# Three products of a hybrid decoder layer turned: weights as the 512-column moving operand, results turned back by TensorE transposes

## The chip, the core and the metric

The kernel runs on one NeuronCore of a Trainium2 chip. The metric is device time in microseconds for one execution; the figure for a kernel is the median of its runs. Before the change three runs took 1487.34, 1488.31 and 1488.09 us, median 1488.09 us.

## What is computed

One decoder layer in float32, for 256 tokens of width 2048. Attention runs inside one block of 256 tokens, with 8 heads of 128; the reference, cut to what matters here:

```python
h = rms_norm(r, g_mix)
z = h @ w_in                                   # 2048 x 10240
q, k, v, c_b, c_c, c_x, g_a, g_c = split(z)    # six of 1024 columns, two of 2048
attn = moba_attention(rms_norm(q), rms_norm(k), v)
y_attn = attn @ w_attn_out                     # 1024 x 2048
y_conv = (c_b * causal_depthwise_conv(c_c * c_x, w_conv)) @ w_conv_out
merged = sigmoid(g_a) * y_attn + sigmoid(g_c) * y_conv
r = r + merged @ w_o                           # 2048 x 2048
h = rms_norm(r, g_mlp)
r = r + square(relu(h @ w_up)) @ w_down        # 2048 x 8192, 8192 x 2048
h = rms_norm(r, g_ple)
r = r + sigmoid(h @ w_ple_gate) * (p @ w_ple_proj)
```

## The kernel before

A float32 product is made from three passes: weights and activations are each split into a high part (a rounding write, ScalarE, L87) and a low part (VectorE subtracts, L88), and TensorE adds up high times high, high times low and low times high.

Weights come from HBM in **units** of 128 x 2048 floats (1 MB), one DMA each on the SyncE queue (`load_unit`, L119), into three `raw` buffers. A unit is split in two halves of 1024 columns; `w_hi` and `w_lo` have seven half-unit buffers each. A unit is what 16 pairs of 128 x 128 weight tiles need.

There are two forms of product.

- `cols` (L155 to L160) keeps features on partitions. A tile of 128 weight columns is stationary. For each of its 16 steps `mm` issues a **pair**: the high weights over [x_hi | x_lo], 512 columns (L150, the last step L153), and the low weights over x_hi, 256 columns (L151). One bank then holds two parts of a result of 128 features x 256 tokens, which `total` or `add_to_r` adds up.
- `rows` (L127 to L143) keeps tokens on partitions. The activations are stationary and the split weights move, 512 columns in each instruction: three matmuls (L139, L140, L141) for each of 16 steps and each of two halves of the tokens, so 96 for a **chunk** of 512 weight columns. The result is two banks of 128 tokens x 512 features.

Before the change `rows` makes q, k and v (six chunks, about the first 147 us), and `cols` all else, in this order: convolution inputs (`ps_conv`), for each of 16 tiles the two gates and the two branch outputs (`ps_g`, `ps_y`), w_o (`ps_o`), then four times a quarter of w_up (`ps_up`) and of w_down (`ps_dn`), at last the per-layer gate (`ps_pg`, `ps_proj`).

In the gate stage a gate's tile is added up by ScalarE and VectorE (L163, L164), multiplied by the norm's row (L343) and put through the sigmoid (L344); a branch output is added up the same way and multiplied by its gate (L352); the two are added (L354) and split into the operand `mT` of w_o (L87, L88). For w_down `add_to_r` adds both parts of each tile to the residual `r` on VectorE (L363, 128 instructions for the four quarters).

Six PSUM banks serve the products (`acc`) and two the small work of attention, such as transposes (`trp`, tag `tr`). Functions in the list `pending` are called between weight units of a product (`run_pending`); attention's pieces, one group of four transposes (`tr_qk`, L263) and others, run in that way within the q, k and v products. The framework's scheduler fixes the order on each engine when the program is built, and each engine then runs its instructions in that order.

Of the kernel before, what the change touches and what calls it, by code (L numbers as in the profile page):

```python
# [29 lines left out]
# Rows of the packed per-channel vectors, as columns after the load.  # L30
# [5 lines left out]
def hybrid_block_kernel(ctx: ExitStack, tc: tile.TileContext, ins: dict, out: bass.AP):  # L36
    """A float32 matrix product runs as three float32r passes: each operand is the exact sum of a
    high and a low part of 12 bits (a float32r write rounds to the high one), and
    hi*hi + hi*lo + lo*hi leaves out only what lies below float32's last bit.

    q, k and v come out with tokens on partitions: weights are the moving operand. All else is kept
    transposed, features on partitions: a tile of 128 weight columns is the stationary operand, its
    high part over [x_hi | x_lo] (512 columns), its low part over x_hi. A norm's 1/rms is applied to a
    product's result, its gain to the operand."""
# [31 lines left out]
    def col(i):  # L76
        return vec[:, i:i + 1]

    def rsqrt_mean(dst, sumsq, n, k):
        """dst = (sumsq / n + eps) ** -0.5 on [128, k]."""  # L80
        nc.vector.tensor_scalar(dst, sumsq, 1.0 / n, EPS, op0=ALU.mult, op1=ALU.add)
        nc.gpsimd.tensor_tensor(dst, dst, half[:, :k], op=ALU.pow)

    def split(hi, lo, src, gain=None):
        """hi + lo = src * gain, exactly."""
# [7 lines left out]
    def xsplit(xs, k, src, gain=None):  # L93
        """xs[k] = [hi | lo] of 128 features."""
# [21 lines left out]
    def load_unit(w):  # L116
        """A unit of 128 x 2048 weights, split, in halves."""
# [9 lines left out]
    def rows(wname, c, xs, name, load=load_unit, pops=1):  # L127
        """Two banks: [256 tokens, 512] of xs @ w, chunk c of w's columns."""
        w = ins[wname]
        nu = w.shape[1]  # L130
        ps = [bank(f"ps_{name}_{t}") for t in range(NT)]
        for u in range(nu):
            wt = load(w[c, u])
# [10 lines left out]

    def mm(ps, wt, i, x, first, last):
        """Tile i of a unit's 16 against x: ps[:, :256] += hi * hi, ps[:, 256:] += the cross products."""
# [8 lines left out]
    def cols(wt, xs, name, at=0, nk=16):  # L155
        """One bank: two parts of [128, 256 tokens] of (xs @ w) transposed."""
        ps = bank(f"ps_{name}")
        for k in range(nk):
            mm(ps, wt, at + k, xs[k], k == 0, k == nk - 1)
        return ps  # L160
# [40 lines left out]
    def load_first(w):  # L201
        """A unit of weights and as much of x, in the order in which the first product needs them."""
# [100 lines left out]
    for c in range(2):  # L303
        if c == 0:
            ps_q = rows("w_qkv", 0, xT, "q0", load_first)
            x_stats()
            ps_k = rows("w_qkv", 2, xT, "k0", pops=3)
            qs[c], ks[c] = qk_evac(ps_q, "q0"), qk_evac(ps_k, "k0")
        else:
            qs[c] = qk_evac(rows("w_qkv", 1, xT, "q1"), "q1")  # L310
            ks[c] = qk_evac(rows("w_qkv", 3, xT, "k1"), "k1")
        vs[c] = tokens(rows("w_qkv", 4 + c, xT, f"v{c}"), f"v{c}")
# [24 lines left out]
    mT = {}  # L337
    for n in range(16):
        gates = []
        for i in range(2):  # L340
            g = temp(f"g{i}")
            total(g, cols(load_unit(w_in[24 + 16 * i + n]), xT, f"g{i}_{n}"))
# [163 lines left out]
```

## Time and profile before

| what | value |
|---|---|
| runs | 1487.34, 1488.31, 1488.09 us; median 1488.09 |
| span of the profiled execution | 1486.1 us |
| the profiled execution's own time | not listed apart; by the median of the runs, 2.0 us lie outside the span |
| TensorE busy | 1475.5 us, 99% |
| VectorE busy | 959.9 us, 65% |
| ScalarE busy | 755.5 us, 51% |
| DMA | 278.46 MB, mean 187 GB/s |
| granted TensorE clock | 1.000 |

The span runs from the first to the last instruction. A TensorE record is longer than the distance to the next one's start, because matmuls overlap; what a matmul costs in a stream is the distance from start to start. Busy time is the union of the records.

### The profile page before, as it was taken

How to read it: one execution, taken by the hardware profiler on the slowest of the kernel's cores; microseconds unless marked ns; L12 is line 12 of the kernel's file. 1: busy time of each engine (PE TensorE's matmuls, PEld its weight loads, DVE VectorE, ACT ScalarE, POOL GpSimd, SP SyncE). 2: the span in 40 equal slices, each digit the busy share in tenths (PEclk: the TensorE clock that was granted, in tenths of full speed). 3: DMA queues.
4: the chain of work that ended last, by engine and by line, in shares of the span. 5: the costliest groups of instructions: out<-in, count | busy, mean ns of one | idle time of the engine just before them, and what ended most of it. 6: DMA issues, size and time to landing. Idle time of an engine off the chain costs nothing.

```text
span 1486.1 us, 20573 instructions
## 1 busy us (share of the span) xinstructions
PE 1475.5 (99%) x8216; PEld 1275.9 (86%) x8216; DVE 959.9 (65%) x1352; ACT 755.5 (51%) x1135; POOL 11.2 (1%) x27
## 2 busy tenths in 40 slices
PE   8999999999999999999999999999999999999998
PEld 6888888888888888888888888888888888888887
DVE  7555676766666666666655666556665566677775
ACT  7655555455555544445543455334553345554543
POOL 0100000000000000000000000000000000000000
PEclk9999999999999999999999999999999999999999
DMA  8545444454545556454545555454555555455551
GB/s 314 225 170 181 173 177 176 173 187 181 198 172 197 180 189 246 180 189 178 198 174 195 180 189 189 180 198 173 196 179 189 189 180 198 173 195 185 191 199 57
DMA packets 44304, 278.46 MB, mean 187 GB/s; under 512 B 5040, under 2 KB 7344, under 8 KB 11952
## 3 DMA queue, kind: packets, MB, share of 16 engines
q1 hardware_dynamic: 44064, 277.11, 51.5%
q8 instruction: 65, 1.06, 0.3%
q14 instruction: 31, 0.25, 0.0%
q10 hardware_dynamic: 144, 0.04, 0.0%
HBM read 275.03 MB, written 2.10 MB: 186 GB/s over the span
## 4 chain that ended last, share of the span: by engine, by line
PE 99%; DMA 0%; DVE 0%; ACT 0%; issue 0%
PE ps_dn L150 15%; PE ps_up L150 15%; PE ps_dn L151 8%; PE ps_up L151 8%; PE ps_g L150 8%; PE ps_conv L150 6%; PE ps_g L151 4%; PE ps_o L150 4%; PE ps_pg L150 4%; PE ps_y L150 4%; PE ps_conv L151 3%; PE ps_o L151 2%; PE ps_pg L151 2%; PE ps_y L151 2%; PE ps_q L139 1%; PE ps_q L141 1%
## 5 line engine op out<-in xcount | busy, mean ns | idle before, releaser
L88 DVE TENSOR_TENSOR w_lo<-raw,w_hi 128x1024 fp32r<-128x1024 f32 (+1 forms) x524 | 632.2, 1208 | 281.8 <-ACT w_hi L87 272.9
L87 ACT ACTIVATE w_hi<-raw 128x1024 fp32r<-128x1024 f32 (+1 forms) x524 | 547.0, 1045 | 402.5 <-PE ps_dn L153 121.6
L150 PE MATMUL ps_up<-x,w_hi 128*128 128x512 f32 x960 | 341.7, 399 | 0.0
L150 PE MATMUL ps_dn<-x,w_hi 128*128 128x512 f32 x960 | 341.7, 399 | 0.0
L151 PE MATMUL ps_dn<-x,w_lo 128*128 128x256 f32 x1024 | 277.2, 281 | 0.0
L151 PE MATMUL ps_up<-x,w_lo 128*128 128x256 f32 x1024 | 277.1, 281 | 0.0
L150 PEld LDWEIGHTS ps_dn<-x,w_hi 128*128 128x128 f32 x960 | 180.4, 188 | 41.6
L150 PEld LDWEIGHTS ps_up<-x,w_hi 128*128 128x128 f32 x960 | 180.4, 188 | 41.5
L151 PEld LDWEIGHTS ps_dn<-x,w_lo 128*128 128x128 f32 x1024 | 193.3, 189 | 6.4
L151 PEld LDWEIGHTS ps_up<-x,w_lo 128*128 128x128 f32 x1024 | 193.3, 189 | 6.3
L150 PE MATMUL ps_g<-x,w_hi 128*128 128x512 f32 x480 | 170.9, 399 | 0.0
L151 PE MATMUL ps_g<-x,w_lo 128*128 128x256 f32 x512 | 138.6, 281 | 0.0
L150 PE MATMUL ps_conv<-x,w_hi 128*128 128x512 f32 x360 | 129.5, 402 | 0.0
L150 PEld LDWEIGHTS ps_g<-x,w_hi 128*128 128x128 f32 x480 | 90.2, 188 | 20.8
L151 PE MATMUL ps_conv<-x,w_lo 128*128 128x256 f32 x384 | 103.5, 280 | 0.0
L151 PEld LDWEIGHTS ps_g<-x,w_lo 128*128 128x128 f32 x512 | 96.7, 189 | 3.2
L163 ACT ACTIVATE a<-ps_up 128x256 f32<-128x256 f32 x64 | 24.6, 384 | 119.8 <-PE ps_up L153 119.8
L150 PE MATMUL ps_o<-x,w_hi 128*128 128x512 f32 x240 | 85.4, 399 | 0.0
L150 PE MATMUL ps_pg<-x,w_hi 128*128 128x512 f32 x240 | 85.4, 398 | 0.0
L363 DVE TENSOR_TENSOR r<-ps_dn,r 128x256 f32<-128x256 f32 x128 | 54.3, 424 | 42.9 <-PE ps_dn L153 40.7
L150 PEld LDWEIGHTS ps_conv<-x,w_hi 128*128 128x128 f32 x360 | 67.6, 188 | 15.3
L150 PE MATMUL ps_y<-x,w_hi 128*128 128x512 f32 x224 | 80.4, 398 | 0.0
(181 smaller groups left out, 1657.8 us busy)
## 6 DMA issues: line engine op xcount, KB each, us to landing
raw<-in_w_up_dram SPq DMA_DIRECT2D x64, 1024.0 KB, 4.8
raw<-in_w_down_dram SPq DMA_DIRECT2D x64, 1024.0 KB, 4.8
raw<-in_w_in_dram SPq DMA_DIRECT2D x56, 1024.0 KB, 4.8
raw<-in_w_qkv_dram SPq DMA_DIRECT2D x20, 1024.0 KB, 4.8
raw<-in_w_branch_dram SPq DMA_DIRECT2D x16, 1024.0 KB, 4.8
raw<-in_w_o_dram SPq DMA_DIRECT2D x16, 1024.0 KB, 4.8
raw<-in_w_ple_gate_dram SPq DMA_DIRECT2D x16, 1024.0 KB, 4.9
raw<-in_w_qkv_dram SPq DMA_DIRECT2D x16, 256.0 KB, 6.1
```

The lines of the kernel that those rows point to most:

```text
L87: nc.scalar.activation(hi, src, AF.Copy)
L88: nc.vector.tensor_sub(lo, src, hi.bitcast(F32))
L139: nc.tensor.matmul(ps[t], xh, hi, start=k == 0, stop=False)
L141: nc.tensor.matmul(ps[t], xl, hi, start=False, stop=k == KU * nu - 1)
L150: nc.tensor.matmul(ps, wh, both, start=first, stop=False)
L151: nc.tensor.matmul(ps[:, S:], wl, x[:, 0, :], start=False, stop=False)
L163: nc.scalar.activation(dst, ps[:, S:], AF.Copy)
L363: nc.vector.tensor_add(dst, ps[:, i * S:(i + 1) * S], dst)
```

## The change

The gates, the branch outputs and the product with w_down go from `cols` to `rows`. w_in, w_branch and w_down still lie in HBM as tiles of 128 columns, so a unit is now gathered from four neighbouring tiles, a quarter of each, by one DMA of 128 x 4 x 512 (`load_rows`), and split in four pieces of 512 columns: ScalarE and VectorE read four runs of 128 columns and write 512 in a row. The gates are read from PSUM by one sigmoid with the norm's factor as scale, tokens being on partitions; VectorE multiplies the branch outputs by them and adds. The merge is turned back by TensorE transposes (`transposed`, groups of four) and split into `mT` from PSUM. The four quarters of w_down add up in eight tiles `d`; after the last quarter `d` is transposed and added to `r`, and the operand `hP` and the sum of squares `ss2` follow. `cols` has a new argument `flush`: at step 12 of a tile the queued work is run, for the first tile of w_o and of the per-layer gate.

```diff
+    def load_rows(w):
+        raw = wp.tile([P, UNIT], F32, tag="raw", name="raw", bufs=3)
+        nc.sync.dma_start(raw.rearrange("p (n f) -> p n f", n=4), w.rearrange("n p f -> p n f"))
+        src = raw.rearrange("p (n k m) -> p k n m", n=4, k=KU)
+        halves = []
+        for h in range(2):
+            hi = wp.tile([P, HALF], F32R, tag="hi", name="w_hi")
+            lo = wp.tile([P, HALF], F32R, tag="lo", name="w_lo")
+            view = [t.rearrange("p (k n m) -> p k n m", n=4, k=2) for t in (hi, lo)]
+            for j in range(2):
+                split(view[0][:, j], view[1][:, j], src[:, 2 * h + j])
+            halves.append((hi, lo))
+        return halves
...
+    def tiles(wname, n, us=range(4)):
+        w = ins[wname]
+        return [lambda u=u: load_rows(w[n:n + 4, :, u * CW:(u + 1) * CW]) for u in us]
...
-    def cols(wt, xs, name, at=0, nk=16):
+    def cols(wt, xs, name, at=0, nk=16, flush=None):
         ps = bank(f"ps_{name}")
         for k in range(nk):
+            if k == flush:
+                run_pending(len(pending))
             mm(ps, wt, at + k, xs[k], k == 0, k == nk - 1)
...
+    def transposed(n, src, done):
+        ps = trp.tile([P, 2, S], F32, tag="tr", name=f"tr_{n}")
+        for i in range(2):
+            o = (n + i) % 4 * P
+            for t in range(NT):
+                nc.tensor.transpose(ps[:, i, t * P:(t + 1) * P], src[t][:, o:o + P], ident)
+        done(n, ps)
...
+    def split_m(n, ps):
+        for i in range(2):
+            xsplit(mT, n + i, ps[:, i, :])
+
+    for c in range(4):
         gates = []
         for i in range(2):
-            g = temp(f"g{i}")
-            total(g, cols(load_unit(w_in[24 + 16 * i + n]), xT, f"g{i}_{n}"))
-            nc.vector.tensor_mul(g, g, row0)
-            nc.scalar.activation(g, g, AF.Sigmoid)
+            ps = rows(tiles("w_in", 24 + 16 * i + 4 * c), xT, f"g{i}_{c}", pops=2)
+            g = [slot([P, CW], F32, f"g{i}_{c}_{t}") for t in range(NT)]
+            for t in range(NT):
+                nc.scalar.activation(g[t], ps[t], AF.Sigmoid, scale=st0["col"][:, t:t + 1])
             gates.append(g)
-            run_pending(len(pending))
-        wt = load_unit(ins["w_branch"][n])
-        parts = []
+        run_pending(len(pending))
         for i, xs in enumerate((attnT, convT)):
-            y = temp(f"y{i}")
-            total(y, cols(wt, xs, f"y{i}_{n}", at=8 * i, nk=8))
-            nc.vector.tensor_mul(y, y, gates[i])
-            parts.append(y)
-        nc.vector.tensor_add(parts[0], parts[0], parts[1])
-        xsplit(mT, n, parts[0])
+            ps = rows(tiles("w_branch", 4 * c, range(2 * i, 2 * i + 2)), xs, f"y{i}_{c}")
+            for t in range(NT):
+                nc.vector.tensor_mul(gates[i][t], ps[t], gates[i][t])
+        for t in range(NT):
+            nc.vector.tensor_add(gates[0][t], gates[0][t], gates[1][t])
+        for n in (4 * c, 4 * c + 2):
+            pending.append(lambda n=n, m=gates[0]: transposed(n, m, split_m))
...
-        add_to_r(n, cols(load_unit(ins["w_o"][n]), mT, f"o_{n}"))
+        add_to_r(n, cols(load_unit(ins["w_o"][n]), mT, f"o_{n}", flush=12))
...
+    def end_r(n, ps):
+        u = n // 2
+        nc.vector.tensor_add(r[u], ps, r[u])
+        for i in range(2):
+            xsplit(hP, n + i, r[u][:, i, :], col(G_PLE + n + i))
+        square_sum(ss2, u, r[u])
...
-        for n in range(16):
-            add_to_r(n, cols(load_unit(ins["w_down"][16 * q + n]), uT, f"dn_{q}_{n}"))
+        for c in range(4):
+            ps = rows(tiles("w_down", 16 * q + 4 * c), uT, f"dn_{q}_{c}")
+            for t in range(NT):
+                if q == 0:
+                    d[c, t] = slot([P, CW], F32, f"d_{c}_{t}")
+                    nc.scalar.activation(d[c, t], ps[t], AF.Copy)
+                else:
+                    nc.vector.tensor_add(d[c, t], ps[t], d[c, t])
             if q == 3:
-                xsplit(hP, n, r[n // 2][:, n % 2, :], col(G_PLE + n))
-                if n % 2 == 1:
-                    square_sum(ss2, n // 2, r[n // 2])
+                for n in (4 * c, 4 * c + 2):
+                    pending.append(lambda n=n, m=(d[c, 0], d[c, 1]): transposed(n, m, end_r))
...
-        gate = cols(wt, hP, f"pg_{n}")
+        gate = cols(wt, hP, f"pg_{n}", flush=12)
```

A group of four transposes turns 256 columns of both token halves. There are 16 groups: eight for the merge, eight for `d`. How the instructions then stand is shown at three places.

**ScalarE, at the end of a gate's product.** `w_hi<-raw` is a split of weights, `g` a gate; xN is a run of N like rows. Before, the last gate of tile 4 and the branch outputs behind it:

```order
L163 ACTIVATE g_3239<-ps_g_4_3250 128x256
L87 ACTIVATE w_hi<-raw 128x1024
L344 ACTIVATE g_3239<-g_3239 128x256
L87 ACTIVATE w_hi<-raw 128x1024
L163 ACTIVATE g_3287<-ps_g_4_3298 128x256
L87 ACTIVATE w_hi<-raw 128x1024
L344 ACTIVATE g_3287<-g_3287 128x256
L163 ACTIVATE y_3345<-ps_y_4_3346 128x256
L87 ACTIVATE w_hi<-raw 128x1024
L163 ACTIVATE y_3366<-ps_y_4_3367 128x256
```

Now, the two gates of chunk 1:

```order
L88 ACTIVATE x<-tr_3160 128x256 x2
L88 ACTIVATE w_hi<-raw 128x512 x10
L383 ACTIVATE g_1_0_3285<-ps_g_1_0_3109,rstd_mix 128x512
L383 ACTIVATE g_1_1_3286<-ps_g_1_1_3110,rstd_mix 128x512
L88 ACTIVATE w_hi<-raw 128x512 x16
L383 ACTIVATE g_1_0_3443<-ps_g_1_0_3289,rstd_mix 128x512
L383 ACTIVATE g_1_1_3444<-ps_g_1_1_3290,rstd_mix 128x512
```

Each split is half as long, and a gate is read once, by a sigmoid of 128 x 512 for each token half, behind ten (then sixteen) quarter splits since the last such stop. Counted over the whole list, when a product's result is read, splits for at least three units (six halves) behind that product stand ahead of the reader, before as now, on ScalarE and on VectorE.

**TensorE, in the first tile of w_o.** `ps_o_4636` is that tile, `ps_o_4706` the second, `tr_4661` and `tr_4672` are the last two groups of transposes of the merge; twelve steps of the first tile stand ahead of the piece. Before, from the end of the first tile (`ps_o_5090`) to the second:

```order
L151 MATMUL ps_o_5090<-x,w_lo 128x256
L150 MATMUL ps_o_5090<-x,w_hi 128x512
L151 MATMUL ps_o_5090<-x,w_lo 128x256 x2
L153 MATMUL ps_o_5090<-x,w_hi 128x512
L150 MATMUL ps_o_5138<-x,w_hi 128x512
L151 MATMUL ps_o_5138<-x,w_lo 128x256
```

Now:

```order
L368 MATMUL tr_4661<-ident,g_3_1_4286 128x128
L368 MATMUL tr_4672<-ident,g_3_0_4285 128x128
L368 MATMUL tr_4672<-ident,g_3_1_4286 128x128
L368 MATMUL tr_4672<-ident,g_3_0_4285 128x128
L368 MATMUL tr_4672<-ident,g_3_1_4286 128x128
L173 MATMUL ps_o_4706<-x,w_hi 128x512
L174 MATMUL ps_o_4706<-x,w_lo 128x256
L173 MATMUL ps_o_4706<-x,w_hi 128x512
L173 MATMUL ps_o_4636<-x,w_hi 128x512
L174 MATMUL ps_o_4636<-x,w_lo 128x256
L174 MATMUL ps_o_4706<-x,w_lo 128x256
```

Before, the sixteen steps of a w_o tile stood in one row. Now its last four wait until the merge has been transposed and split, and one or two steps of the second tile stand between them.

**VectorE, from the last chunk of w_down to the first tile of the per-layer gate.** `d` is the sum of the quarters, `tr_11359` and `tr_11374` its last transposes, `ss` the sum of squares. Before, from the last tile but one of w_down to the gate's first tile:

```order
L363 TENSOR_TENSOR r_5077<-ps_dn_14_12011,r_5077 128x256 x2
L88 TENSOR_TENSOR w_lo<-raw,w_hi 128x1024
L91 SCALAR_TENSOR_TENSOR x<-r_5077,vec,x 128x256
L88 TENSOR_TENSOR w_lo<-raw,w_hi 128x1024
L363 TENSOR_TENSOR r_5077<-ps_dn_15_12059,r_5077 128x256 x2
L88 TENSOR_TENSOR w_lo<-raw,w_hi 128x1024
L91 SCALAR_TENSOR_TENSOR x<-r_5077,vec,x 128x256
L176 TENSOR_TENSOR ss_5870<-ss_5870,sq 128x512
L88 TENSOR_TENSOR w_lo<-raw,w_hi 128x1024
```

Now:

```order
L451 TENSOR_TENSOR d_0_6898<-ps_dn_3_0_11124,d_0_6898 128x512
L451 TENSOR_TENSOR d_1_6900<-ps_dn_3_1_11125,d_1_6900 128x512
L89 TENSOR_TENSOR w_lo<-raw,w_hi 128x1024 x2
L422 TENSOR_TENSOR r_4621<-tr_11359,r_4621 128x512
L422 TENSOR_TENSOR r_4623<-tr_11374,r_4623 128x512
L92 SCALAR_TENSOR_TENSOR x<-r_4621,vec,x 128x256 x2
L201 TENSOR_TENSOR ss_5438<-ss_5438,sq 128x512
L92 SCALAR_TENSOR_TENSOR x<-r_4623,vec,x 128x256 x2
L201 TENSOR_TENSOR ss_5438<-ss_5438,sq 128x512
```

Behind the last product there stood two additions to `r` for one tile, its split and one sum of squares. Now there are two additions to `d`, two weight splits, two additions to `r` of 512 columns, four splits and two sums of squares, and the last four steps of the gate's first tile wait for them.

## Rows read from the trace of the kernel before

**Rows 1.** The page: span, busy time, TensorE and its clock in 40 slices.

```profile
span 1486.1 us, 20573 instructions
...
PE 1475.5 (99%) x8216; PEld 1275.9 (86%) x8216; DVE 959.9 (65%) x1352; ACT 755.5 (51%) x1135; POOL 11.2 (1%) x27
...
PE   8999999999999999999999999999999999999998
...
PEclk9999999999999999999999999999999999999999
```

**Rows 2.** Waits of TensorE, all: us in total, times, longest.

```profile
PE ps_q L139 <- ACT x L90: 5.8, 1, 5.8
```

**Rows 3.** TensorE timeline, `cols`, first quarter of w_down: start, duration, engine, line.

```profile
745.11 0.40 PE L150 MATMUL ps_dn<-x,w_hi 128*128 128x512 f32 x1
745.34 0.28 PE L151 MATMUL ps_dn<-x,w_lo 128*128 128x256 f32 x1
745.45 0.40 PE L150 MATMUL ps_dn<-x,w_hi 128*128 128x512 f32 x1
...
834.84 0.40 PE L150 MATMUL ps_dn<-x,w_hi 128*128 128x512 f32 x1
835.08 0.40 PE L151 MATMUL ps_dn<-x,w_lo 128*128 128x256 f32 x2
835.32 0.40 PE L153 MATMUL ps_dn<-x,w_hi 128*128 128x512 f32 x1
835.56 0.40 PE L150 MATMUL ps_up<-x,w_hi 128*128 128x512 f32 x1
```

**Rows 4.** TensorE timeline, `rows`: first chunk of v, 96 matmuls, to the next chunk.

```profile
53.58 0.40 PE L140 MATMUL ps_v<-w_lo,x 128*128 128x512 f32 x1
53.81 0.39 PE L141 MATMUL ps_v<-w_hi,x 128*128 128x512 f32 x1
...
74.89 0.39 PE L141 MATMUL ps_v<-w_hi,x 128*128 128x512 f32 x1
75.12 0.39 PE L139 MATMUL ps_q<-w_hi,x 128*128 128x512 f32 x1
```

**Rows 5.** TensorE timeline, `rows`, around one group of four transposes.

```profile
80.33 0.39 PE L141 MATMUL ps_q<-w_hi,x 128*128 128x512 f32 x1
80.56 0.38 PE L263 MATMUL tr_qk<-ident,q 128*128 128x128 f32 x2
80.78 0.38 PE L263 MATMUL tr_qk<-ident,k 128*128 128x128 f32 x2
80.92 0.48 PE L139 MATMUL ps_q<-w_hi,x 128*128 128x512 f32 x1
81.23 0.40 PE L140 MATMUL ps_q<-w_lo,x 128*128 128x512 f32 x1
81.47 0.40 PE L141 MATMUL ps_q<-w_hi,x 128*128 128x512 f32 x1
81.70 0.39 PE L139 MATMUL ps_q<-w_hi,x 128*128 128x512 f32 x1
81.93 0.39 PE L140 MATMUL ps_q<-w_lo,x 128*128 128x512 f32 x1
```

**Rows 6.** Groups by line, splits and a four-run read: busy, mean ns, idle.

```profile
L88 DVE TENSOR_TENSOR w_lo<-raw,w_hi 128x1024 fp32r<-128x1024 f32 x508 | 621.3, 1224 | 274.8 <-ACT w_hi L87 265.9
L88 DVE TENSOR_TENSOR w_lo<-raw,w_hi 128x512 fp32r<-128x512 f32 x16 | 10.8, 690 | 7.0 <-ACT w_hi L87 7.0
L250 DVE TENSOR_TENSOR k<-k,rinv_k 128x512 f32<-128x512 f32 x4 | 2.6, 689 | 3.6 <-POOL rinv_k L82 3.6
L87 ACT ACTIVATE w_hi<-raw 128x1024 fp32r<-128x1024 f32 x508 | 537.1, 1058 | 398.1 <-PE ps_dn L153 121.6 <-PE ps_dn L150 90.3 <-PE ps_up L150 36.5
L87 ACT ACTIVATE w_hi<-raw 128x512 fp32r<-128x512 f32 x16 | 10.0, 627 | 4.3 <-DMA raw<-in_w_qkv_dram 4.1
```

**Rows 7.** Groups by line: the readers of results, VectorE and ScalarE.

```profile
L363 DVE TENSOR_TENSOR r<-ps_dn,r 128x256 f32<-128x256 f32 x128 | 54.3, 424 | 42.9 <-PE ps_dn L153 40.7
L91 DVE SCALAR_TENSOR_TENSOR x<-r,vec,x 128x256 fp32r<-128x256 f32 x32 | 15.3, 479 | 0.0
L176 DVE TENSOR_TENSOR ss<-ss,sq 128x512 f32<-128x512 f32 x21 | 14.4, 684 | 0.7 <-ACT sq L175 0.7
L90 ACT ACTIVATE x<-r,vec 128x256 fp32r<-128x256 f32 x32 | 15.8, 493 | 0.0
L235 ACT ACTIVATE v<-ps_v,rstd_mix 128x512 f32<-128x512 f32 x4 | 2.6, 690 | 1.0 <-PE ps_v L141 1.0
L87 ACT ACTIVATE x<-ps_o 128x256 fp32r<-128x256 f32 x8 | 3.0, 372 | 0.0
```

**Rows 8.** DMA issues: KB each, median us from issue to landing.

```profile
raw<-in_w_down_dram SPq DMA_DIRECT2D x64, 1024.0 KB, 4.8
raw<-in_w_qkv_dram SPq DMA_DIRECT2D x16, 256.0 KB, 6.1
```

**Rows 9.** Window: busy PE, PEld, DVE, ACT, POOL; clock, DMA share, GB/s.

```profile
10.00:15.00 5.00, 5.00 (x20) 4.03 (x20) 4.00 (x8) 4.42 (x9) 0.00 (x0) 1.00 1.04 392
```

**Rows 10.** SyncE queue timeline, w_o and residual loads: start, us first to last.

```profile
534.59 28.91 SPq L119 DMA_DIRECT2D raw<-in_w_o_dram  x6
563.55 4.79 SPq L367 DMA_DIRECT2D r<-in_xT_dram  x8
568.70 0.33 SPq L119 DMA_DIRECT2D raw<-in_w_o_dram  x1
```

More of the change, by code (lines that the diff above doesn't have):

```diff
@@ L125, in load_half, with rows @@
         return split_half(raw)
-    def rows(wname, c, xs, name, load=load_unit, pops=1):
-        w = ins[wname]
-        nu = w.shape[1]
+    def load_rows(w):
[11 more added lines that the diff above has]
+        return halves
+    def rows(units, xs, name, pops=1):
+        nu = len(units)
         ps = [bank(f"ps_{name}_{t}") for t in range(NT)]
-        for u in range(nu):
-            wt = load(w[c, u])
+        for u, load in enumerate(units):
+            wt = load()
             for j in range(KU):
@@ L143, in rows, with qkv @@
         return ps
+    def qkv(c, load=load_unit):
+        return [lambda u=u: load(ins["w_qkv"][c, u]) for u in range(4)]
+    def tiles(wname, n, us=range(4)):
+        w = ins[wname]
+        return [lambda u=u: load_rows(w[n:n + 4, :, u * CW:(u + 1) * CW]) for u in us]
     def mm(ps, wt, i, x, first, last):
@@ L304, in hybrid_block_kernel @@
         if c == 0:
-            ps_q = rows("w_qkv", 0, xT, "q0", load_first)
+            ps_q = rows(qkv(0, load_first), xT, "q0")
             x_stats()
-            ps_k = rows("w_qkv", 2, xT, "k0", pops=3)
+            ps_k = rows(qkv(2), xT, "k0", pops=3)
             qs[c], ks[c] = qk_evac(ps_q, "q0"), qk_evac(ps_k, "k0")
         else:
-            qs[c] = qk_evac(rows("w_qkv", 1, xT, "q1"), "q1")
-            ks[c] = qk_evac(rows("w_qkv", 3, xT, "k1"), "k1")
-        vs[c] = tokens(rows("w_qkv", 4 + c, xT, f"v{c}"), f"v{c}")
+            qs[c] = qk_evac(rows(qkv(1), xT, "q1"), "q1")
+            ks[c] = qk_evac(rows(qkv(3), xT, "k1"), "k1")
+        vs[c] = tokens(rows(qkv(4 + c), xT, f"v{c}"), f"v{c}")
         for h in range(4 * c, 4 * c + 4):
@@ L379, in hybrid_block_kernel @@
     ss2 = slot([P, 2, S], F32, "ss2")
+    d = {}
+    def end_r(n, ps):
[4 more added lines that the diff above has]
+        square_sum(ss2, u, r[u])
     for q in range(4):
@@ L396, in hybrid_block_kernel @@
             ready = []
-        for n in range(16):
-            add_to_r(n, cols(load_unit(ins["w_down"][16 * q + n]), uT, f"dn_{q}_{n}"))
+        for c in range(4):
[6 more added lines that the diff above has]
+                    nc.vector.tensor_add(d[c, t], ps[t], d[c, t])
             if q == 3:
-                xsplit(hP, n, r[n // 2][:, n % 2, :], col(G_PLE + n))
-                if n % 2 == 1:
-                    square_sum(ss2, n // 2, r[n // 2])
+                for n in (4 * c, 4 * c + 2):
+                    pending.append(lambda n=n, m=(d[c, 0], d[c, 1]): transposed(n, m, end_r))
     praw = slot([P, 2, S], F32, "p")
```

## The prediction, made before the changed kernel had run

> **What bounds the kernel now.** I read the page first: TensorE is busy 1475.5 of 1486.1 us, 99%, nine tenths or more in 38 of 40 slices, and its granted clock is full (1.000, the 2.4 GHz level) throughout; VectorE stands at 65%, ScalarE at 51% [rows 1]. The waits of TensorE come next, because a busy engine may still be starved: there is one wait in the whole run, 5.8 us for the first split of x [rows 2]. So nothing that the other engines save is worth anything by itself. The time is the stream of TensorE instructions, and the question is what one matmul costs in it. The records say 0.40 us for 512 columns, but they overlap, so I take distances from start to start out of the timeline.
>
> **The two forms, priced.** In `cols` the first quarter of w_down starts at 745.11 and the next product at 835.56 [rows 3]: 90.45 us for 16 tiles of 16 pairs, 0.3533 us a pair (0.23 for the 512 columns, 0.11 to 0.12 for the 256). In `rows` 95 matmuls of 512 columns lie between 53.58 and 75.12 [rows 4]: 21.54 us, 0.2267 us each. A pair moves 768 columns, so does one matmul and a half: 0.340 us against 0.3533. Both forms move the same columns; `rows` does it in 96 long matmuls a chunk where `cols` needs 128, half of them short.
>
> Per chunk of 512 weight columns and 2048 of depth: 64 x 0.3533 = 22.61 us before, 96 x 0.2267 = 21.77 now, 0.846 saved. The change turns 8 chunks of gates, 4 of branch outputs (two half-depth products each) and 16 of w_down (four quarters of 2048 columns): 28 x 0.846 = **23.7 us saved**, all of it on the path, as TensorE is the path.
>
> **What the change adds to TensorE.** Sixteen groups of four transposes. The trace has the same group in the q product [rows 5]: from 80.56 to 81.23 there pass 0.67 us with one matmul in it, so 0.44, and the next distances (0.24, 0.23) are 0.02 too long: 0.46 a group. Where two groups follow each other the first costs only its own 0.36 (80.56 to 80.92), so 0.82 for both. The order has five doubles (four in the merge, the last for `d`) and six singles: 5 x 0.82 + 6 x 0.46 = **6.9 us**. The bounds are nothing, if they hid behind other matmuls as weight loads do, which rows 5 speak against, and 16 x 0.46 = 7.4.
>
> **What it adds as waits: two places.** The last merge groups and the last `d` groups stand at step 12 of the next product's first tile, 12 x 0.353 = 4.2 us behind the end of the product that feeds them.
> - First tile of w_o. VectorE has two multiplications and two additions of 128 x 512, at 0.69 each [rows 6] 2.8 us, done by about 3.0 us. The two groups run from 4.2 to 5.1. ScalarE needs 0.37 us for the first high part [rows 7], VectorE 0.42 for the low one (as its other reads of 128 x 256 from PSUM [rows 7]), but two weight splits of 1.22 us [rows 6] stand ahead of it, the second held until the tile's first eight steps have freed a buffer at 2.8 and ScalarE has split at 3.9. VectorE is through them at 5.4 and the low part is there at 5.9. TensorE has one step and a half of the second tile to do, until 5.7: a wait of about 0.25. The three later operands come every 0.45 us, the steps between take longer.
> - First tile of the per-layer gate. VectorE: two additions to `d` until 1.6, a weight split, another until 5.2, two additions to `r` until 6.6, then low parts at 0.48 [rows 7] at 7.1, 7.6, 8.8 and 9.2 with a sum of squares of 0.68 [rows 7] between. TensorE meanwhile does the transposes (to 5.1), the projection (0.7) and three steps of the second tile (1.1), until 6.8, then waits 0.3 and twice 0.1: 0.5. The matmuls on the sum of squares stand two steps further back.
>
> Together **0.8 us**, between nothing and 11.6: both chains with nothing beside them, two splits of 1.22 at either place, 2.1 us for four operands in the first, 2 x 0.69 + 4 x 0.48 + 2 x 0.68 = 4.7 in the second. I take the worked value, since it counts what stands between.
>
> **What costs nothing, and what hides it.**
> - Splits in quarters: a unit costs VectorE 4 x 0.690 = 2.76 instead of 2 x 1.224 = 2.45 us, ScalarE 4 x 0.627 = 2.51 instead of 2.12 [rows 6]; over 112 units 35 and 44 us more. A unit lasts TensorE 21.77 / 4 = 5.44 us, so both engines stay near half busy. That the source is now four runs of 128 costs no more by the nearest row: VectorE's read of a 128 x 512 tile as four runs, L250, takes 689 ns, the plain one 690 [rows 6]. Uncovered, the price is double: 5.5 us on VectorE, just above 5.44.
> - Readers of results: gone are 128 additions of 0.424 in w_down, 54 us, and the sums of the gates and branches; new are reads of 512 columns at 0.69 (L235) [rows 7]. All wait at a product's end with six split halves, three units or 16 us, ready ahead of them; before it was the same lead and no wait of TensorE came of it [rows 2].
> - Loads: still one of 1 MB per unit, 112 of them in runs of 2 KB instead of 8. A unit's load landed in 4.8 us [rows 8]. The first product's loads have 2 KB runs too, 256 KB each; queued behind each other they landed in 6.1 us [rows 8], and the stretch at 10 to 15 us moved 392 GB/s [rows 9]. Needed are 1.05 MB in 5.44 us, 193 GB/s.
> - The eight loads of `r` on the SyncE queue stood behind six w_o loads and left from 563.55 to 568.34 [rows 10]; now they stand behind two, and the other w_o loads behind them. They wait for operands of the last gate, free some 22 us before w_o begins. With three `raw` buffers the third w_o load has more than 16 us to its use, so a 4.8 us longer queue is covered; uncovered it would be those 4.8 us once.
>
> **Sum.** -23.7 + 6.9 + 0.8 = -16.0 us. The span goes from 1486.1 to 1470.1; the runs' median lies 2.0 above the span, and I leave that: 1488.1 - 16.0 = **1472.1 us**.
>
> **A rule against the sum.** The Trainium skill, page "TensorE: Matmul & The Clock Gate", section "Back-to-back issue gap", states that matmuls in a row start N / 2.4 + 2.5 ns apart at the full clock. By it a pair is 325.0 ns and a long matmul 215.8, a chunk 20.80 us before and 20.72 now; the change would save 28 x 0.08 = 2.2 us, pay 7.7 and end at 1493.6. The trace does not agree: 353.3 and 226.7 ns, so a fixed cost of each matmul well above that page's, and a short one pays it too.
>
> **The rivals.**
> 1. *The price hangs on the stretch, not on the form.* `rows` was seen only in the first 147 us. If a long matmul in the gates and w_down costs its share of today's pair, 2/3 x 0.3533 = 0.2355 us, the saving is nil and the additions remain: 1488.1 + 7.7 = **1495.8**, slower. It decides at 0.2327 us a matmul: there 28 x (22.61 - 96 x 0.2327) pays the 7.7. For it: right behind a group of transposes the distance is 0.233 on average (81.23 to 81.93) [rows 5], just that value. Against it: 95 in a row hold 0.2267 [rows 4], with the same operand shapes and the same clock. The skill's rule above is its neighbour. Chance 0.06.
> 2. *The two places wait in full.* VectorE or ScalarE come to the transposed results late, and 11.6 us stand in place of 0.8: **1482.9**, still faster. For it: the lists put two weight splits ahead of the results. Against: the gap of 4.2 us was worked out with them. Chance of half of it or more, 0.10.
> 3. *The splits set the pace.* If the four-run source costs VectorE double, a unit takes it 4 x 1.38 = 5.52 us and the readers 0.35 (two of 0.69 in four units), 5.87 instead of 5.44: 112 x 0.43 = 48 us on top of 1472.1, **1520**, slower. L250 [rows 6] speaks against it. Chance 0.03, and 0.01 more for loads of under 193 GB/s.
> 4. *The transposes cost nothing*: 1488.1 - 23.7 + 0.8 = **1465.2**. Rows 5 show the gap in the stream. Chance 0.03.
>
> **How the numbers follow.** The forecast has 0.77; the rivals have the rest. A measurement of this kernel can tell about 0.2%, 3 us, from no change. The range runs from 1465, the free transposes, to 1480, three quarters of the way to rival 2's price; left out are rivals 1 and 3 and the worst of rival 2, some 0.13. Faster by more: forecast, rivals 2 and 4, **0.90**. Slower by more: rivals 1 and 3, less what lies between, **0.07**. Within: **0.03**, rival 1 near its deciding point.
>
> **What would show it.** Start to start in the gates and w_down 0.227 us and a quarter of w_down near 87.1 us instead of 90.45, if right; 0.233 or more, and rival 1 holds. Each group of transposes opens 0.36 to 0.46 us in the stream. TensorE's waits should stay near 6 us; entries at the first tile of w_o and of the gate above 0.5 us are rival 2, waits on `w_hi` or `w_lo` within a product are rival 3, with L89 well over 690 ns, or the loads, with a landing time over 10 us. The forecast is wrong if the quarter of w_down isn't shorter, or if it is and the gain is lost at the two places.

## The result, and the profile after

| | before | after |
|---|---|---|
| median of the runs, us | 1488.11 (1487.34 to 1488.31, 4 runs) | 1472.16 (1471.48 to 1472.83, 4 runs) |
| span of the profiled execution, us | 1486.1 | 1470.1 |
| ratio of the times, 95% interval | | 0.9893 [0.9879, 0.9907] |

The changed kernel is 1.07% faster, 15.95 us. The forecast was 1472.1.

The page of the changed kernel, its lines that answer to [rows 1] and [rows 8]:

```profile
span 1470.1 us, 18933 instructions
...
PE 1459.7 (99%) x7384; PEld 1237.6 (84%) x7384; DVE 895.6 (61%) x1360; ACT 757.8 (52%) x1287; POOL 11.2 (1%) x27
...
PEclk9999999999999999999999999999999999999999
...
raw<-in_w_down_dram SPq DMA_DIRECT2D x64, 1024.0 KB, 5.1
raw<-in_w_in_dram SPq DMA_DIRECT2D x56, 1024.0 KB, 5.0
...
raw<-in_w_ple_gate_dram SPq DMA_DIRECT2D x16, 1024.0 KB, 5.1
```

TensorE is at 99% as before; the share tells nothing of the gain. It issues 832 instructions fewer and its clock is as before. A unit gathered from four tiles lands in 5.0 to 5.1 us, against 4.8 [rows 8]; units of the per-layer gate, which aren't gathered, take 5.1 in this run too (4.9 before), so not all of the 0.2 to 0.3 is the gathering's.

All waits of TensorE and of its weight loads after the change (us in total, times, longest):

```profile
PE ps_q L154 <- ACT x L91: 5.6, 1, 5.6
```

```profile
PEld ps_q L154 <- ACT x L91: 5.8, 2, 5.6
PEld ps_q L156 <- DVE x L92: 0.3, 1, 0.3
PEld ps_o L173 <- DVE x L89: 0.2, 1, 0.2
PEld ps_pg L173 <- DVE x L92: 0.2, 1, 0.2
```

The first wait is the one of [rows 2]. The two last lines are the two places that the prediction worked out, and the list shows no other wait there.

Where the time went is read from the starts of the products. TensorE's timeline after the change, at the edges of the gate stage, of the first quarter of w_down and of the last:

```profile
292.01 0.40 PE L154 MATMUL ps_g<-w_hi,x 128*128 128x512 f32 x1
...
555.81 0.39 PE L173 MATMUL ps_o<-x,w_hi 128*128 128x512 f32 x1
...
738.76 0.40 PE L154 MATMUL ps_dn<-w_hi,x 128*128 128x512 f32 x1
...
825.81 0.39 PE L173 MATMUL ps_up<-x,w_hi 128*128 128x512 f32 x1
...
1271.24 0.40 PE L154 MATMUL ps_dn<-w_hi,x 128*128 128x512 f32 x1
...
1361.21 0.39 PE L173 MATMUL ps_pg<-x,w_hi 128*128 128x512 f32 x1
```

The first quarter of w_down takes 825.81 - 738.76 = 87.05 us for 384 matmuls, 0.2267 each; in [rows 3] it took 90.45. The same edges in TensorE's timeline of before, beside [rows 3] (gate stage, w_o, last quarter of w_down, per-layer gate):

```profile
292.03 0.40 PE L150 MATMUL ps_g<-x,w_hi 128*128 128x512 f32 x1
...
563.17 0.40 PE L150 MATMUL ps_o<-x,w_hi 128*128 128x512 f32 x1
...
1287.82 0.40 PE L150 MATMUL ps_dn<-x,w_hi 128*128 128x512 f32 x1
...
1378.28 0.40 PE L150 MATMUL ps_pg<-x,w_hi 128*128 128x512 f32 x1
```

With these, stage by stage:

| stage, start to start | before | after | difference | by the prediction's terms |
|---|---|---|---|---|
| gates and branches (12 chunks, 3 double groups) | 271.14 | 263.80 | -7.34 | -10.15 + 2.46 = -7.69 |
| w_o (1 double group, 1 wait) | 90.45 | 91.47 | +1.02 | 0.82 + 0.25 = +1.07 |
| w_down, first three quarters together | 271.36 | 261.14 | -10.22 | -10.15 |
| w_down, last quarter (6 single groups) | 90.46 | 89.97 | -0.49 | -3.38 + 2.76 = -0.62 |
| per-layer gate to its third tile (1 double group, 1 wait) | 13.87 | 14.93 | +1.06 | 0.82 + 0.5 = +1.32 |
| sum | | | -15.97 | -16.07 |

The rest of the program, the w_up product among it, is as long as before. The table closes on the 16.0 us that the span lost.

### The profile page after: what moved, and what is told of

It reads as the page before. It is cut to its first block, busy times and chain, and to the rows that moved or that the text cites. A ratio compares the mean times of both kernels' runs of the same rounds, so it can differ in the third digit from the quotient of the medians.

```text
span 1470.1 us, 18933 instructions
## 1 busy us (share of the span) xinstructions
PE 1459.7 (99%) x7384; PEld 1237.6 (84%) x7384; DVE 895.6 (61%) x1360; ACT 757.8 (52%) x1287; POOL 11.2 (1%) x27
## 4 chain that ended last, share of the span: by engine, by line
PE 99%; DMA 0%; DVE 0%; ACT 0%; issue 0%
PE ps_up L173 15%; PE ps_up L174 8%; PE ps_dn L156 8%; PE ps_dn L154 8%; PE ps_dn L155 8%; PE ps_conv L173 6%; PE ps_g L156 4%; PE ps_g L154 4%; PE ps_g L155 4%; PE ps_o L173 4%; PE ps_pg L173 4%; PE ps_conv L174 3%; PE ps_o L174 2%; PE ps_pg L174 2%; PE ps_y L156 2%; PE ps_y L154 2%
## 5 line engine op out<-in xcount | busy, mean ns | idle before, releaser
L89 DVE TENSOR_TENSOR w_lo<-raw,w_hi 128x512 fp32r<-128x512 f32 (+1 forms) x748 | 647.8, 892 | 412.1 <-ACT w_hi L88 407.1
L88 ACT ACTIVATE w_hi<-raw 128x512 fp32r<-128x512 f32 (+1 forms) x748 | 568.6, 789 | 474.1 <-PE ps_dn L156 173.9
L154 PE MATMUL ps_dn<-w_hi,x 128*128 128x512 f32 x512 | 199.8, 390 | 0.0
L156 PE MATMUL ps_dn<-w_hi,x 128*128 128x512 f32 x512 | 199.3, 389 | 0.0
L155 PE MATMUL ps_dn<-w_lo,x 128*128 128x512 f32 x512 | 199.2, 389 | 0.0
L156 PEld LDWEIGHTS ps_dn<-w_hi,x 128*128 128x128 f32 x512 | 96.1, 188 | 20.2
L155 PEld LDWEIGHTS ps_dn<-w_lo,x 128*128 128x128 f32 x512 | 96.1, 188 | 20.0
L154 PEld LDWEIGHTS ps_dn<-w_hi,x 128*128 128x128 f32 x512 | 96.1, 188 | 19.4
L154 PE MATMUL ps_g<-w_hi,x 128*128 128x512 f32 x256 | 99.9, 390 | 0.0
L156 PE MATMUL ps_g<-w_hi,x 128*128 128x512 f32 x256 | 99.6, 389 | 0.0
L155 PE MATMUL ps_g<-w_lo,x 128*128 128x512 f32 x256 | 99.6, 389 | 0.0
L174 PEld LDWEIGHTS ps_conv<-x,w_lo 128*128 128x128 f32 x384 | 72.5, 189 | 1.4
```

The source lines that it names most:

```text
L88: nc.scalar.activation(hi, src, AF.Copy)
L89: nc.vector.tensor_sub(lo, src, hi.bitcast(F32))
L154: nc.tensor.matmul(ps[t], xh, hi, start=k == 0, stop=False)
L155: nc.tensor.matmul(ps[t], xh, lo, start=False, stop=False)
L156: nc.tensor.matmul(ps[t], xl, hi, start=False, stop=k == KU * nu - 1)
L174: nc.tensor.matmul(ps[:, S:], wl, x[:, 0, :], start=False, stop=False)
```

## The experiments

**What stood open.** The total fits the forecast, but a sum can fit with two wrong terms. So the first runs take the change apart: the gates alone, w_down alone, and all of it without the transposes. My theory: a chunk saves 0.85 us wherever it stands, the transposes stand in the stream and cost 6.9 us, the waits little. The rivals are those of the prediction: the price hangs on the stretch, or the transposes are free.

The second question is why a pair costs more than a matmul and a half. Theory A: every matmul pays a fixed amount, long or short. From 0.3533 = 1.5 x 0.2267 + half of that amount it would be 26.5 ns. Theory B: a short matmul by itself costs about half a long one, and the change from one length to the other costs the rest. A and B say the same of the change itself, and different things of other kernels.

### e1_gates: the gates and branches turned, w_down as before

Against the changed kernel:

```diff
-        for c in range(4):
-            ps = rows(tiles("w_down", 16 * q + 4 * c), uT, f"dn_{q}_{c}")
...
+        for n in range(16):
+            add_to_r(n, cols(load_unit(ins["w_down"][16 * q + n]), uT, f"dn_{q}_{n}"))
```

> Only the gates and branch outputs are turned; w_down stays in the old form. Theory (the saving is the price of the stream, chunk by chunk): 12 chunks x 0.846 = 10.2 us saved, four double groups of transposes 4 x 0.82 = 3.3 and a wait of 0.2 at the first tile of w_o given back: -6.7 us, about 1481.4, and the w_down quarters stay at 90.45 us. Rival (the saving comes from the lighter load on the other engines, not from the form): the parts don't add up with those of the other half, and the old quarters of w_down change too.

Measured: 1481.46 us (1480.91 to 1482.03) beside 1487.74 for the kernel before, ratio 0.9959 [0.9946, 0.9971]. Its gate stage runs from 292.24 to 556.04, 263.80 us, the same as in the full change; its first quarter of w_down from 738.98 to 829.43, 90.45, as before.

### e2_down: w_down turned, the gates and branches as before

Against the kernel before (the edit of the gate stage, undone here, isn't shown):

```diff
-        for n in range(16):
-            add_to_r(n, cols(load_unit(ins["w_down"][16 * q + n]), uT, f"dn_{q}_{n}"))
+        for c in range(4):
+            ps = rows(tiles("w_down", 16 * q + 4 * c), uT, f"dn_{q}_{c}")
...
```

The gate stage stays that of the kernel before.

> Only the product with w_down is turned; gates and branch outputs stay in the old form. Theory: 16 x 0.846 = 13.5 us saved, six single groups and one double, 2.8 + 0.8 = 3.6, and waits of 0.3 at the gate's first tile given back: -9.6 us, about 1478.5; together with the other half this gives the whole change. Rival as there.

Measured: 1478.75 us, ratio 0.9939 [0.9925, 0.9953]. Gate stage 271.14 us as before, first quarter of w_down from 745.39 to 832.44, 87.05. The two parts save 0.41% and 0.61%, together 1.02%, against 1.07% for both at once: within the intervals they add up. What one part does is not undone by the other: each stage has the length that it has in the full change.

### e3_unturned: the transposes left out

The merge and the sum of w_down aren't turned back: the operands are made from the same buffers with tokens on partitions, so this kernel leaves the transposition out of the computation.

```diff
-        ps = trp.tile([P, 2, S], F32, tag="tr", name=f"tr_{n}")
-        for i in range(2):
-            o = (n + i) % 4 * P
-            for t in range(NT):
-                nc.tensor.transpose(ps[:, i, t * P:(t + 1) * P], src[t][:, o:o + P], ident)
-        done(n, ps)
+        done(n, src[n // 2 % 2].rearrange("p (k s) -> p k s", s=S))
```

> The changed kernel without the transposes: the merge and the sum of the quarters are split and added as they lie, tokens on partitions, so the turning is left out of the computation. Theory (transposes stand in the stream): 6.9 us less than the changed kernel, and up to 0.5 of the waits at the two places gone too, so 1464.8 to 1465.3. Rival (transposes hide behind other matmuls): no change from 1472.

Measured: 1463.74 us (1463.53 to 1464.28), ratio 0.9840 [0.9827, 0.9853]; 8.4 us less than with the transposes, about one more than I expected; span 1461.9. TensorE's timeline of this kernel, at the edges of the gate stage and of the last quarter of w_down:

```profile
291.58 0.40 PE L154 MATMUL ps_g<-w_hi,x 128*128 128x512 f32 x1
...
552.71 0.39 PE L173 MATMUL ps_o<-x,w_hi 128*128 128x512 f32 x1
...
1267.11 0.40 PE L154 MATMUL ps_dn<-w_hi,x 128*128 128x512 f32 x1
...
1354.16 0.39 PE L173 MATMUL ps_pg<-x,w_hi 128*128 128x512 f32 x1
```

The gate stage is 261.13 us instead of 263.80: its three double groups cost 2.67, 0.89 each. The last quarter is 87.05, as the first ones, instead of 89.97: six single groups cost 2.92, 0.49 each. w_o takes 90.44 instead of 91.47, so the double group there and the wait behind it are 1.03; the head of the per-layer gate 13.73 instead of 14.93, so 1.20. These two are sums of a double group and a wait; if each of these doubles costs 0.89 as well, the waits are 0.14 and 0.31. Transposes 7.4 us, waits 0.45, together 7.8; 0.4 us of the 8.2 between the spans lies ahead of the gate stage (291.58 against 292.01), where the two kernels have the same instructions.

### e4_grouped: matmuls of one length together

Where `cols` still stands (1888 pairs) the order within a tile is changed: eight long, sixteen short, eight long, and the same again in the next tile, so that runs of sixteen follow each other. No matmul is added or dropped.

```diff
+        if nk == 16 and not (flush is not None and pending):
+            for g in range(2):
+                ks = range(8 * g, 8 * g + 8)
+                for low in ((0, 1), (1, 0))[g]:
+                    for k in ks:
...
```

> The changed kernel, and in all products that are still in the old form (but the first tiles of w_o and of the per-layer gate) the order of a tile's matmuls is changed: eight long ones, sixteen short ones, eight long ones, in place of long and short in turn; 1888 pairs are concerned. Theory A (every matmul has its own fixed cost, whatever stands beside it; from 0.2267 us and 0.3533 us a pair that is 0.027 us and 0.39 ns a column): a pair stays 0.353 us, no change from 1472. Theory B (the turn from long to short is what the old form pays for): a pair falls, at most to the 0.340 us that the same columns cost in long matmuls: up to 25 us less, and at least 3.

Measured: 1463.95 us (1463.39 to 1464.23), ratio 0.9840 [0.9827, 0.9854], 8.2 us less than the changed kernel. TensorE's timeline, three runs within w_up and the edges of its second quarter:

```profile
700.22 3.82 PE L190 MATMUL ps_up<-x,w_hi 128*128 128x512 f32 x16
703.88 2.08 PE L188 MATMUL ps_up<-x,w_lo 128*128 128x256 f32 x16
705.79 2.46 PE L190 MATMUL ps_up<-x,w_hi 128*128 128x512 f32 x10
...
822.50 0.39 PE L190 MATMUL ps_up<-x,w_hi 128*128 128x512 f32 x1
...
911.57 0.39 PE L154 MATMUL ps_dn<-w_hi,x 128*128 128x512 f32 x1
```

The quarter takes 89.07 us for 256 pairs, 0.3479 a pair, against 90.45 and 0.3533 in the changed kernel. Sixteen short ones take 705.79 - 703.88 = 1.91, 0.1194 each; sixteen long ones 3.66, 0.2288 each. The same matmuls in another order cost 1.5% less: theory A alone can't give that. By 1888 x 0.0054 it would be 10.2 us; not every stretch gains it whole. The convolution inputs, with pieces of attention between their tiles, gain 0.4 us (145.10 to 144.71 from their first start to the gates') instead of 2.1, the first quarter of w_up 1.0 (91.48 to 90.46) instead of 1.4; why isn't shown. And 0.7 of the 8.2 us lies ahead of the first reordered tile (146.23 against 146.91), where both kernels have the same instructions: differences of under a microsecond between two kernels are read from their stages here, not from their times.

### e5_before_grouped: nothing turned, the grouped order in every tile

The kernel before, with `cols` ordered as in e4 (the half-depth branch tiles in groups of four).

```diff
-        for k in range(nk):
-            mm(ps, wt, at + k, xs[k], k == 0, k == nk - 1)
+        h = nk // 2
+        for g in range(2):
+            for low in ((0, 1), (1, 0))[g]:
+                for k in range(h * g, h * g + h):
...
```

> The kernel before, nothing turned, only the order of the matmuls in each tile changed: long ones, then the short ones, then long ones (in the half-depth branch products four, eight, four). Theory B, with the prices read from the grouped run (0.228 us a long one, 0.119 a short one, 0.348 a pair against 0.3533): 3456 pairs of whole tiles x 0.0056 = 19.4 us and about 1.3 from the branch products: about 1467.4, so faster than the turned kernel. Rival (the saving of the grouped run belongs to its stretches or to the turned kernel's balance of engines): less than 8 us, about 1480 or more.

Measured: 1470.25 us (1469.98 to 1470.55), ratio 0.9882 [0.9869, 0.9896]. That is 2.9 us above the time expected. Most of what is missing lies in the first half of the kernel: by the starts of the products the convolution inputs gain 0.4 us (145.10 to 144.71) instead of 2.2, the gate stage 3.6 (271.14 to 267.51) instead of 4.2, the first quarter of w_up 1.0 instead of 1.4; why isn't shown. But the order saves 17.4 us, and without a transpose, a gathered load or a new buffer it is as fast as the change. Its first quarter of w_down, from its timeline:

```profile
737.87 0.39 PE L170 MATMUL ps_dn<-x,w_hi 128*128 128x512 f32 x1
...
826.94 0.39 PE L170 MATMUL ps_up<-x,w_hi 128*128 128x512 f32 x1
```

89.07 us again, where the turned form needs 87.05. So against a well-ordered `cols` the turned form saves (89.07 - 87.05) / 4 = 0.50 us a chunk: 28 x 0.50 = 14.1, less 7.8 for transposes and waits, 6.3. The runs say 1470.25 - 1463.95 = 6.3.

### e6_pairs: groups of two

As e4, with two long and two short by turns, so that runs of four follow each other.

```diff
-            for g in range(2):
-                ks = range(8 * g, 8 * g + 8)
-                for low in ((0, 1), (1, 0))[g]:
+            for g in range(8):
+                ks = range(2 * g, 2 * g + 2)
+                for low in ((0, 1), (1, 0))[g % 2]:
...
```

> As the grouped run on the changed kernel, in groups of two: two long, four short, four long, four short and so on, so 8 changes of length in a tile instead of 32 in the changed kernel and 2 in the grouped one. Theory B, each change of length costing the same (0.09 us a tile for 30 of them, 0.003 each): 24 of 30 parts of the 8.2 us, 6.6 less than 1472.2, so 1465.6. Rival (only long runs of one length help): 1470 or more.

Measured: 1468.27 us, ratio 0.9868 [0.9855, 0.9882]: 3.9 us less than the changed kernel where an equal price for each change of length says 6.6. The timeline within w_up:

```profile
700.18 1.09 PE L190 MATMUL ps_up<-x,w_hi 128*128 128x512 f32 x4
701.11 0.63 PE L188 MATMUL ps_up<-x,w_lo 128*128 128x256 f32 x4
701.58 1.09 PE L190 MATMUL ps_up<-x,w_hi 128*128 128x512 f32 x4
```

Four long ones take 0.93, 0.2325 each, four short ones 0.47. The expectation miscounted by two: the changed kernel has 30 changes of length in a tile, so an equal price says 22 of 28 parts of 8.2, or 6.4 us; that isn't there either.

Where the loss lies can be read from the single starts in the second quarter of w_up. Mean distance to the next start, in ns:

| order | long ones, by their place behind the short ones | long, mean | short, mean |
|---|---|---|---|
| changed kernel, long and short by turns | 236 | 236.2 | 117.1 |
| e6, runs of four | 234, 234, 232, 228 | 232.3 | 118.5 |
| e4, runs of sixteen | 233, 235, 228, 232, 231, then 227 | 228.4 | 119.5 |
| long ones alone [rows 4] | | 226.7 | |

Against the last line a turn from short to long costs 0.010 us where long and short alternate (0.007 net, since the short one is 2 ns quicker there), 0.022 in runs of four and 0.026 in runs of sixteen. So the price isn't paid at one matmul: it lies on the first five long ones behind the turn, and alternation cuts it short but pays at every pair. What holds them up isn't visible in the records.

### e7_short: the long matmuls of w_up cut in two

All but the first and the last long one of a w_up tile become two of 256 columns, in the order of before, so that nearly all matmuls there have one length.

```diff
+                    nc.tensor.matmul(ps[:, :S], wh, xs[k][:, 0, :], start=False, stop=False)
+                    nc.tensor.matmul(ps[:, S:], wh, xs[k][:, 1, :], start=False, stop=False)
...
```

> The changed kernel, and in w_up each long matmul but the first and last of a tile is issued as two short ones of 256 columns: 896 pairs become triples of short ones, the same columns. Theory A (a fixed cost of 0.027 us for each matmul, 0.39 ns a column): a triple is 0.380 us, +23.9 us, 1496. Theory B (0.1194 us for a short one beside short ones): 0.358 us, +4.4 us, about 1476.6.

Measured: 1477.02 us (1476.59 to 1477.48), ratio 0.9927 [0.9914, 0.9941], 4.9 us more than the changed kernel. Of theory A's 24 us a fifth is there; theory B's number holds. In the timeline:

```profile
700.79 0.27 PE L189 MATMUL ps_up<-x,w_hi 128*128 128x256 f32 x1
700.90 0.28 PE L190 MATMUL ps_up<-x,w_hi 128*128 128x256 f32 x1
701.02 0.28 PE L191 MATMUL ps_up<-x,w_lo 128*128 128x256 f32 x1
701.14 0.28 PE L189 MATMUL ps_up<-x,w_hi 128*128 128x256 f32 x1
```

Each short one takes 0.12, whichever half of the operand it reads. The changes between `w_hi` and `w_lo` and between the halves of the bank are the same here as in the changed kernel, and the short ones stand 0.120 apart all the same; which leaves the change of length as what the alternating order pays for. Two short ones cost 2 x 0.1194 - 0.2267 = 0.012 us more than one long: that is what one more matmul costs together with its weight load, half of what theory A needs. Which of the two it is, no run shows: every matmul here has a weight load of its own, and among short ones the loads stand 0.120 apart as well. Less the 0.007 of a change of length saved, a cut costs 0.005; for the 64 tiles of w_up with 14 cuts each 4.5 us, near the 4.9 measured.

### e8_flush4: the queued work at step 4 instead of step 12

The transposes at the first tile of w_o and of the per-layer gate come earlier, so that the merge or the sum has less time and the operands behind them more.

```diff
-        add_to_r(n, cols(load_unit(ins["w_o"][n]), mT, f"o_{n}", flush=12))
+        add_to_r(n, cols(load_unit(ins["w_o"][n]), mT, f"o_{n}", flush=4))
...
-        gate = cols(wt, hP, f"pg_{n}", flush=12)
+        gate = cols(wt, hP, f"pg_{n}", flush=4)
```

> The changed kernel with the queued transposes called at step 4 instead of 12 of the first tile of w_o and of the per-layer gate, so about 1.8 us behind the product that feeds them (the order has five or six steps ahead of them). Theory (step 12 is what covers the additions): at w_o the additions are through at 3.0 us and TensorE waits about 1.2 us; at the gate two additions are through at 1.6 and nothing is waited for at the transposes; behind them little changes, as more steps follow: about 1 us more, 1473. Rival (the place does not matter, or the waits are hidden by other steps): no wait in the trace, 1472.

Measured: 1471.44 us (1471.20 to 1471.82), ratio 0.9890 [0.9877, 0.9904]; the changed kernel stands at 0.9893 [0.9879, 0.9907]. The wait that I expected isn't there. TensorE's timeline in the first tile of w_o:

```profile
557.12 0.40 PE L173 MATMUL ps_o<-x,w_hi 128*128 128x512 f32 x1
557.45 0.41 PE L368 MATMUL tr<-ident,g 128*128 128x128 f32 x2
557.62 0.36 PE L174 MATMUL ps_o<-x,w_lo 128*128 128x256 f32 x1
557.82 0.40 PE L173 MATMUL ps_o<-x,w_hi 128*128 128x512 f32 x1
558.06 0.82 PE L368 MATMUL tr<-ident,g 128*128 128x128 f32 x6
558.63 0.36 PE L174 MATMUL ps_o<-x,w_lo 128*128 128x256 f32 x1
```

The eight transposes stand apart here: two for the first half of the tokens, then a pair of the product's matmuls, then the other six. The distance from 557.12 to 557.45 holds about 0.1 us more than usual. w_o takes 91.43 us instead of 91.47, the head of the per-layer gate 14.65 instead of 14.93. So the place of the transposes, step 4 or step 12, makes 0.3 us in all, and the small waits behind them stay: TensorE's weight loads still wait 0.2 us at either place.

### e10_grouped_flush4: e4 and e8 together

Both edits above.

> The grouped run with the queued transposes called at step 4 of the two first tiles, as in the run on the place. If the two gains are independent: 8.2 and 0.7 us below the changed kernel, 1463.3. If the call at step 4 only filled gaps that the grouped order closes too: 1463.9 as the grouped run.

Measured: 1463.71 us (1463.48 to 1464.15), ratio 0.9837 [0.9824, 0.9851]; e4 has 0.9840 [0.9827, 0.9854]. The two can't be told apart; the gain is that of the grouped order. These are the fastest complete versions, some 24 us under the kernel before and 8 under the change.

## Why the prediction was right, point by point

**The bound.** TensorE's stream is the time before and after, with its one wait of 5.6 to 5.8 us. Nothing in the loads, ScalarE or VectorE showed on the path, though VectorE's busy time fell by 64 us (959.9 to 895.6).

**The price of a chunk.** Forecast 0.846 us saved for each of 28, 23.7 in all. Measured, without transposes: 3.40 us a quarter of w_down, 0.85 a chunk, and with e3's gate stage (271.14 - 261.13) / 12 = 0.83; 23.6 in all. Distances from start to start gave it; the records' own durations (0.40 + 0.28 a pair against 1.5 x 0.40) would have given 0.08 us a pair instead of 0.0133, six times too much.

**The transposes.** They stand in the stream, as [rows 5] had them. TensorE's timeline after the change, around a double group in the gate stage:

```profile
362.51 0.39 PE L156 MATMUL ps_g<-w_hi,x 128*128 128x512 f32 x1
362.74 1.03 PE L368 MATMUL tr<-ident,g 128*128 128x128 f32 x8
363.53 0.48 PE L154 MATMUL ps_g<-w_hi,x 128*128 128x512 f32 x1
363.84 0.40 PE L155 MATMUL ps_g<-w_lo,x 128*128 128x512 f32 x1
```

From 362.51 to 363.84 there pass 1.33 us with two matmuls in it (0.45), so 0.88. Forecast 0.82 for a double and 0.46 for a single, measured 0.89 and 0.49: 7.4 us instead of 6.9. One group in one place [rows 5] was a little too cheap a sample.

**The two waits.** Forecast 0.25 and 0.5; by e3, with 0.89 for the group, 0.14 and 0.31. For w_o, VectorE's timeline after the change shows the chain that was worked out:

```profile
555.53 1.28 DVE L389 TENSOR_TENSOR g<-ps_y,g 128x512 f32<-128x512 f32 x2
556.73 1.28 DVE L391 TENSOR_TENSOR g<-g,g 128x512 f32<-128x512 f32 x2
557.93 1.22 DVE L89 TENSOR_TENSOR w_lo<-raw,w_hi 128x1024 fp32r<-128x1024 f32 x1
559.80 1.23 DVE L89 TENSOR_TENSOR w_lo<-raw,w_hi 128x1024 fp32r<-128x1024 f32 x1 [0.65 <-ACT w_hi L88]
561.10 0.43 DVE L89 TENSOR_TENSOR x<-tr,x 128x256 fp32r<-128x256 f32 x1
```

w_o starts at 555.81. The order is the forecast's: two multiplications, two additions, a weight split, a gap for the buffer, the second split, the low part. One step in it was wrong: the additions were to be through 3.0 us behind the product, they were at 2.2. The first multiplication starts 0.28 before w_o does, since the first bank is complete earlier than the second, and the four stand 0.60 from start to start, not 0.69. It made no difference, because the transposes wait for step 12 at 4.2 us anyway; it is the slip on which my expectation for e8 fell. The low part is there 5.7 us behind (561.53), forecast 5.9, needed from 5.7. What TensorE then loses:

```profile
561.27 0.81 PE L173 MATMUL ps_o<-x,w_hi 128*128 128x512 f32 x2
561.92 0.40 PE L174 MATMUL ps_o<-x,w_lo 128*128 128x256 f32 x2
```

Two long matmuls take 0.65, where 2 x 0.23 is usual: 0.19 too long, and 0.05 more lies a few steps on. That is 0.24 by the rows and 0.14 by e3's difference; the forecast lies at the upper one. At the per-layer gate the same count of starts gives 0.17, 0.05 and 0.08, together 0.30, where the forecast had 0.3 and twice 0.1.

**The errors cancel.** Transposes 0.5 more, waits 0.3 less, chunks 0.1 less, and 0.14 that no term had: without the transposes the head of the per-layer gate is 13.73 us in e3, 13.87 before. The mechanism and its prices held; that the total was right to 0.1 us is luck, since the terms were right to half a microsecond only and the four runs lie 1.35 us apart.

**What was to cost nothing.** The groups of the changed kernel by line, to be read beside [rows 6]:

```profile
L89 DVE TENSOR_TENSOR w_lo<-raw,w_hi 128x512 fp32r<-128x512 f32 x464 | 300.8, 688 | 240.9 <-ACT w_hi L88 240.6
L88 ACT ACTIVATE w_hi<-raw 128x512 fp32r<-128x512 f32 x464 | 268.5, 624 | 273.3 <-PE ps_dn L156 134.8 <-PE ps_g L156 66.6 <-PE ps_y L156 36.9
```

A split of four runs of 128 takes 688 and 624 ns, as the plain one did (690 and 627). ScalarE's idle time there ends with TensorE's matmuls, so the buffers are full and the splits run ahead.

**The rivals.**
1. The price hangs on the stretch: falls. 0.2267 us a matmul in w_down, far from 0.2327, and the gate stage agrees.
2. Both places wait in full: falls. 0.45 us of the 11.6, and e8 moved the place and found 0.1 us of wait at the transposes.
3. The splits set the pace: falls with the two lines above and the landing time of 5.1 us.
4. The transposes are free: falls with e3. Without them the kernel takes 1463.74.

**The step that was only half right** stands behind the sum: "a fixed cost of each matmul ... and a short one pays it too". It has no part in the sum, which went by measured pairs, and so nothing was lost by it; but as a reason it would mislead. By e4, e6 and e7 a pair is 0.2267 for the long, 0.1194 for the short and, net, 0.007 for the change of length. A chunk of 64 pairs is dearer than 96 long matmuls by 64 x (0.1194 - 0.1134) = 0.39 us for short ones and by 64 x 0.007 = 0.46 for the changes. The grouped order takes 0.35 of the 0.46 back, and leaves 0.50 for the turn to win.

The Trainium skill, page "TensorE: Matmul & The Clock Gate", section "Back-to-back issue gap", gives N / 2.4 + 2.5 ns at the full clock, which the prediction took for matmuls in a row; the section calls it the gap of an isolated matmul, and gives about 131 ns for 512 columns in a stream of weight loads and matmuls. An estimate by the formula is 215.8 ns for 512 columns and 109.2 for 256. No stretch here shows any of these: the shortest mean for 512 columns is 226.7 ns, and the short ones have means of 117.1 to 119.5, some 8 to 11 ns above the formula for either length; and the order of the lengths changes them, of which the section says nothing.

## What to carry to other kernels

When one engine is busy 99% of the time, price its instructions by the distance from start to start, for each form and each order, in stretches of a hundred; the busy share was 99% at 1486 us and at 1462. Before rebuilding a product so that it has fewer or more even instructions, try the same instructions in another order: long and short matmuls in runs of sixteen gave here, in a few lines, as much as the turn with its transposes. Then do both, and count every transpose at its full place in the stream.

## What was not expected of the hardware

- The order of matmuls of unlike length costs time with no wait in the records: a pair of 512 and 256 columns is 0.3533 us when they alternate, 0.3508 in runs of four (89.81 us for the second quarter of w_up in e6), 0.3479 in runs of sixteen. The loss lies on the first five long ones behind a turn from short to long (233, 235, 228, 232 and 231 ns in e4, then 227).
- VectorE operations of 128 x 512 one behind the other start 0.60 us apart (four from 555.53 to 557.93), though one alone has a record of 0.69: as on TensorE, the records overlap.
- Transposes of 128 x 128 between long matmuls hold up the stream by 0.49 us for four and 0.89 for eight, 0.11 to 0.12 each, with the granted clock at 1.00. That is about as much as a short matmul of 256 columns.
